# Hyena mixer of a two-layer hybrid block on Trainium2: its first loads moved ahead of attention's, its GpSimd operations moved to VectorE

## The chip, the cores and the metric

The kernel runs on one core of one Trainium2 chip. The metric is the device time of one execution in microseconds (us). The engines are named PE (TensorE), DVE (VectorE), ACT (ScalarE), POOL (GpSimd) and SP (SyncE, which here issues the loads and stores).

## The reference, cut to what matters

Two layers, 1024 latent tokens and 256 context tokens of width 1024, all in float32. In each layer an input projection feeds four mixers side by side: gated DeltaNet (gdn), Hyena, HGRN2 (hgrn) and differential attention. Their outputs are joined, projected, and an MLP follows. In the last layer the context tokens give no output, so its Hyena has the latent part alone. The part that is changed:

```python
def long_conv_bidir(u, h_fwd, h_bwd, skip):
    n, ch = h_fwd.shape
    kern = jnp.concatenate([h_fwd, jnp.zeros((1, ch), jnp.float32), jnp.flip(h_bwd[1:], axis=0)], axis=0)
    kf = jnp.fft.rfft(kern, n=2 * n, axis=0)
    uf = jnp.fft.rfft(u.astype(jnp.float32), n=2 * n, axis=1)
    y = jnp.fft.irfft(uf * kf, n=2 * n, axis=1)[:, :n]
    return (y + u.astype(jnp.float32) * skip.astype(jnp.float32)).astype(u.dtype)

def hyena_mixer(p_lat, p_ctx, conv_w, filt_params, decay, skip, want_ctx):
    def run(t):
        v, x1, x2 = _split(conv_centred(t, conv_w), [W_GROUP] * 3)
        h = hyena_filters(t.shape[1], *filt_params, decay)
        z = x1 * long_conv_bidir(v, h[:, 0, 0], h[:, 1, 0], skip[0])
        return x2 * long_conv_bidir(z, h[:, 0, 1], h[:, 1, 1], skip[1])
    return run(p_lat), (run(p_ctx) if want_ctx else None)
```

## The kernel before, in words

**Stages of a layer.** `run` builds a layer from generators. Each yields a number after every piece of work, its rough cost, and `mix(lead, fill, ratio)` draws as much of `fill` as `ratio` times what `lead` has yielded. The stages: norm and input projection; gdn with the projection as filler; hgrn as lead with `rest()` as filler; attention as lead with what is left of `rest()`; then the tail (output projection and MLP). The instructions are issued in the order in which the generators write them, with a scheduler of the framework that keeps each engine's queue in a fixed order; each engine works through its own queue in order, and so does SP with its DMAs. An instruction that waits holds up all behind it on its engine.

**The filler.** `rest()` is the end of the projection, then attention's first loads (`next(at[0])`), then the first two loads of `mods` (`next(m2)`), then `weave(hyena, m2)`: Hyena, and between its pieces the blocks 16 to 47 of the adaLN parameters. In layer 0 the first blocks of the next layer's parameters and its Hyena filters follow.

**Attention's loads.** `attn` takes a head in four pairs of `q<-dq` and `k<-dk` loads of 64 partitions x 1280 (L1159), eight in all; the next head's are issued at the start of the present one. Its scores are `psc` at L1199.

**mods.** Each block of 128 columns loads a weight tile `modw` (L342, 512 KB, two buffers) and multiplies it with the conditioning vectors: eight matmuls `pmod` (L364), then transposes `pmodT` (L350).

**hgrn.** Its tiles load `k<-khf`, `k<-khb`, `q<-hq`, `it<-i`, `lf` (L1035 to L1043). Its products are `psc` at L1090 and L1096, `po`, `pkv`, `pexp`, and `pfin` at its end.

**Hyena.** `hyena(l)` does a circular convolution by a DFT whose tokens are split into R phases: part "c" (256 context tokens, R = 2, layer 0 alone), then part "l" (1024 latent tokens, R = 4). For a part it loads the bases `bf` and `bi` (L1313; 2 MB each for "l"), the input `u<-yv` (L1457), for each of the two orders a gate `xg` (L1460), and for each block of 128 frequencies the filter's spectrum `ks` (L1476). Both parts use the same buffers. The work for one block of "l": transposes `put` (L1470, once an order), `pF` (L1319, the forward products), a butterfly over phases to `X` (L1497 to L1504), the complex product with `ks` (L1506 to L1511), a second butterfly (L1517 to L1527), `py` (L1534, the way back) and the updates of `u` (L1538 to L1542). There are eight such blocks in the kernel, and two of "c". `V` is DVE and `G` is POOL:

```python
V.tensor_mul(t1, X[:, :, 0], ks[:, :, 0])
G.tensor_mul(t2, X[:, :, 1], ks[:, :, 1])
V.tensor_mul(Y[:, :, 1], X[:, :, 0], ks[:, :, 1])
V.tensor_mul(X[:, :, 0], X[:, :, 1], ks[:, :, 0])
V.tensor_sub(Y[:, :, 0], t1, t2)
V.tensor_add(Y[:, :, 1], Y[:, :, 1], X[:, :, 0])
```

## Time and profile before

| what | value |
|---|---|
| three runs | 4753.67, 4756.74, 4767.21 us; median 4756.74 |
| span of the profiled execution | 4754.4 us |
| that execution's own time | not listed apart from the span; the span lies 2.3 us under the median |
| PE busy | 4150.7 us, 87% |
| DVE busy | 2304.5 us, 48% |
| ACT busy | 1622.4 us, 34% |
| POOL busy | 1079.8 us, 23% |
| HBM read, written | 343.83 MB, 109.48 MB |

The span is one execution of the whole program. The busy times are sums over it, so they say nothing of one stage. In time order: layer 0 has its hgrn up to about 1130 us, its attention from there to about 1640 and its tail to about 2640; layer 1 has hgrn up to about 3620, attention to about 3920, then the tail.

### The profile page before, as it was taken

The page shows a single profiled execution, that of the slowest core. Times are in us where ns is not written, and L with a number is a line of the kernel's source. Part 1 is how long each engine was busy: PE and PEld are TensorE (multiplying, and loading weights), DVE is VectorE, ACT ScalarE, POOL GpSimd, SP SyncE. Part 2 cuts the span into 40 slices and gives each one's busy share as a digit, 9 for nine tenths or more (in the row PEclk, how much of TensorE's full clock was granted, in tenths as well). Part 3 has the DMA queues.
Part 4 walks back from the last instruction along what each step waited for, and adds up shares of the span by engine and source line. Part 5 has one row for each costly group of instructions (what it writes and reads, how often), then busy time and mean ns, then how long its engine had stood idle before and what let it go on. Part 6 is the DMA issues. An engine that isn't in the chain of part 4 may idle for free. (4 is left out here: it accounts for less than half of the span.)

```text
span 4754.4 us, 81740 instructions
## 1 busy us (share of the span) xinstructions
PE 4150.7 (87%) x33446; PEld 3297.6 (69%) x33446; DVE 2304.5 (48%) x4533; ACT 1622.4 (34%) x3165; POOL 1079.8 (23%) x1101
## 2 busy tenths in 40 slices
PE   5977999856578899999999998899847779999999
PEld 2866877644455678888888676677635566788887
DVE  6566556646687333222222567456647873322222
ACT  3454414423335332222122455514413463321222
POOL 1121120000211423333333121111001104433333
PEclk7998999877788899999999999899967889999999
DMA  5236633324224411111111325634342234211112
GB/s 193 91 87 174 187 104 115 97 96 139 87 83 157 149 56 49 40 41 36 41 40 48 103 84 152 193 106 123 98 141 71 86 115 129 66 50 49 48 49 87
DMA packets 381499, 458.65 MB, mean 96 GB/s; under 512 B 137251, under 2 KB 244387, under 8 KB 379076
## 3 DMA queue, kind: packets, MB, share of 16 engines
q1 hardware_dynamic: 379300, 448.43, 30.2%
q0 software_dynamic: 1824, 4.98, 0.4%
q8 instruction: 264, 4.33, 0.4%
q14 instruction: 111, 0.91, 0.1%
HBM read 343.83 MB, written 109.48 MB: 95 GB/s over the span
## 5 line engine op out<-in xcount | busy, mean ns | idle before, releaser
L256 POOL TENSOR_TENSOR wlo<-wraw,whi 128x512 fp32r<-128x512 f32 x360 | 476.7, 1329 | 804.9 <-ACT whi L255 793.0
L255 ACT CAST whi<-wraw 128x512 fp32r<-128x512 f32 (+1 forms) x480 | 296.9, 620 | 955.1 <-PE pt L261 806.8
L1600 DVE SCALAR_TENSOR_TENSOR tx<-pt,mod,tx 128x512 f32<-128x512 f32 (+1 forms) x360 | 250.9, 697 | 710.0 <-PE pt L262 708.5
L262 PE MATMUL pt<-hh,wlo 128*128 128x512 f32 (+1 forms) x1280 | 472.6, 369 | 4.8 <-POOL wlo L256 4.8
L262 PE MATMUL pt<-fh,wlo 128*128 128x512 f32 (+1 forms) x1280 | 473.9, 370 | 0.0
L261 PE MATMUL pt<-fl,whi 128*128 128x512 f32 (+1 forms) x1280 | 472.8, 369 | 0.0
L260 PE MATMUL pt<-fh,whi 128*128 128x512 f32 (+1 forms) x1280 | 472.7, 369 | 0.0
L260 PE MATMUL pt<-hh,whi 128*128 128x512 f32 (+1 forms) x1280 | 472.1, 369 | 0.0
L261 PE MATMUL pt<-hl,whi 128*128 128x512 f32 (+1 forms) x1280 | 472.0, 369 | 0.0
L1636 DVE TENSOR_TENSOR f<-f 128x512 f32<-128x512 f32 (+1 forms) x160 | 151.9, 951 | 623.3 <-ACT f L1635 619.6
L260 PE MATMUL pproj<-hh,whi 128*128 128x512 f32 (+1 forms) x960 | 371.6, 387 | 8.3 <-ACT u L489 6.4
L261 PE MATMUL pproj<-hl,whi 128*128 128x512 f32 (+1 forms) x960 | 362.6, 378 | 0.0
L262 PE MATMUL pproj<-hh,wlo 128*128 128x512 f32 (+1 forms) x960 | 360.7, 376 | 0.0
L261 PEld LDWEIGHTS pt<-fl,whi 128*128 128x128 f32 x1280 | 240.4, 188 | 56.3 <-issue 13.0
L256 POOL TENSOR_TENSOR fl<-f,fh 128x512 fp32r<-128x512 f32 (+1 forms) x160 | 190.6, 1192 | 390.5 <-ACT fh L255 390.5
L262 PEld LDWEIGHTS pt<-hh,wlo 128*128 128x128 f32 x1280 | 241.6, 189 | 46.6 <-POOL wlo L256 5.6
L260 PEld LDWEIGHTS pt<-fh,whi 128*128 128x128 f32 x1280 | 240.5, 188 | 43.4 <-issue 2.3
L262 PEld LDWEIGHTS pt<-fh,wlo 128*128 128x128 f32 x1280 | 240.5, 188 | 43.1 <-issue 1.5
L261 PEld LDWEIGHTS pt<-hl,whi 128*128 128x128 f32 x1280 | 241.8, 189 | 41.0 <-issue 0.8
L260 PEld LDWEIGHTS pt<-hh,whi 128*128 128x128 f32 x1280 | 241.7, 189 | 40.8 <-ACT whi L255 0.3
L260 PEld LDWEIGHTS pproj<-hh,whi 128*128 128x128 f32 x960 | 186.5, 194 | 48.4 <-issue 8.7
L1201 ACT ACTIVATE p<-psc,mx 128x1280 f32<-128x1280 f32 (+1 forms) x144 | 178.0, 1238 | 120.7 <-DVE mx L1200 71.0
(377 smaller groups left out, 8357.1 us busy)
## 6 DMA issues: line engine op xcount, KB each, us to landing
wraw<-mlp_w SPq DMA_DIRECT2D x296, 256.0 KB
modw<-mod_w SPq DMA_DIRECT2D x80, 512.0 KB
wraw<-w_cm SPq DMA_DIRECT2D x88, 256.0 KB
wraw<-w_out SPq DMA_DIRECT2D x64, 256.0 KB
kv<-kvd SPq DMA_DIRECT2D x40, 256.0 KB
k<-dk SPq DMA_DIRECT2D x32, 320.0 KB
bfl<-c_hyfl SPq DMA_DIRECT2D x4, 2048.0 KB
modw<-mod_w SPq DMA_DIRECT2D x4, 2048.0 KB
```

Of the source, the lines that this page charges most:

```text
L255: (hi_eng or nc.scalar.copy)(hi, src)
L256: (lo_eng or nc.gpsimd).tensor_tensor(lo, src, hi.bitcast(F32), ALU.subtract)
L260: nc.tensor.matmul(ps, wh, xh, start=start, stop=False)
L261: nc.tensor.matmul(ps, wh, xl, start=False, stop=False)
L262: nc.tensor.matmul(ps, wl, xh, start=False, stop=stop)
L1201: nc.scalar.activation(p[j], A, AF.Exp, bias=mx[:, j:j + 1], accum_out=sm[:, j:j + 1])
L1600: nc.vector.scalar_tensor_tensor(xm, p, G[:, m, v:v + 1], xm, ALU.mult, ALU.add)
L1636: nc.vector.tensor_mul(f, f, f)
```

## The change

`hyena` gets a first part, up to a new `yield 0`, that issues the first loads of both parts at once: `sk`, and for each part `bf`, `u`, the first `ks`, `bi` and the first `xg`, each into a buffer of its own (`uc`/`ul`, `xgc`/`xgl`, `ksc`/`ksl`). The buffers `t1` and `t2` go. `rest()` takes that first part ahead of attention's loads and of `mods`, then yields 3.0, so that hgrn runs three units ahead before Hyena's work begins. All operations on POOL in `hyena` go to DVE. The complex product writes into `Y` and `X` in place. Four butterflies of 512 become two of 1024, and for "l" the result is in `Y`. Comments are gone, so line numbers shift (`put` is L1487 after, `u` L1466, `xg` L1454, `ks` L1459, `py` L1548, the stores `o<-u` L1558).

```diff
@@ -1446,19 +1446,36 @@
         gp = es.enter_context(tc.tile_pool(name=f"hy{l}", bufs=1, side="right", reuse_waits="tile"))
         sk = gp.tile([128, 4], F32, tag="sk", name="sk")
         nc.sync.dma_start(sk, self.i["hysk"][l])
-        V, G = nc.vector, nc.gpsimd
-        for nm, tok0, n, a, R in (("c", SEQ, CTX, 1, 2), ("l", 0, SEQ, 2, 4)):
-            if (l, nm) not in self.KS:
-                continue
+        V = nc.vector
+        parts = [p for p in (("c", SEQ, CTX, 1, 2), ("l", 0, SEQ, 2, 4)) if (l, p[0]) in self.KS]
+        def gate(nm, od, tok0, n):
+            xg = gp.tile([128, 2, n], F32, tag="xg" + nm, name="xg")
+            nc.sync.dma_start(xg, S["y1" if od == 0 else "y2"][:, :, tok0:tok0 + n])
+            return xg
+        def spectrum(nm, od, k, R):
+            ks = gp.tile([128, R, 2, 256], F32, tag="ks" + nm, name="ks")
+            nc.sync.dma_start(ks, self.KS[l, nm][:, od, k])
+            return ks
+        got = {}
+        for nm, tok0, n, a, R in parts:
+            bf = self.basis(gp, "f", nm)
+            u = gp.tile([128, 2, n], F32, tag="u" + nm, name="u")
+            nc.sync.dma_start(u, S["yv"][:, :, tok0:tok0 + n])
+            ks = spectrum(nm, 0, 0, R)
+            bi = self.basis(gp, "i", nm)
+            got[nm] = bf, bi, u, gate(nm, 0, tok0, n), ks
+        yield 0
+        for nm, tok0, n, a, R in parts:
             tk = slice(tok0, tok0 + n)
             pn = n // R
-            bf, bi = self.basis(gp, "f", nm), self.basis(gp, "i", nm)
-            u = gp.tile([128, 2, SEQ], F32, tag="u", name="u")[:, :, :n]
-            nc.sync.dma_start(u, S["yv"][:, :, tk])
+            bf, bi, u, xg, ks = got[nm]
             for od in range(2):
-                xg = gp.tile([128, 2, SEQ], F32, tag="xg", name="xg")[:, :, :n]
-                nc.sync.dma_start(xg, S["y1" if od == 0 else "y2"][:, :, tk])
+                if od:
+                    xg = gate(nm, od, tok0, n)
                 ut = gp.tile([128, 2, 4, 256], F32, tag="ut", name="ut")
                 for ai in range(a):
                     for b0 in range(0, R, 2):
@@ -1472,19 +1489,16 @@
                         nc.scalar.copy(ut[:, ai, b0:b0 + 2], pv)
                         yield 0.2
                 for k in range(a):
-                    ks = gp.tile([128, 4, 2, 256], F32, tag="ks", name="ks")[:, :R]
-                    nc.sync.dma_start(ks, self.KS[l, nm][:, od, k])
+                    if od or k:
+                        ks = spectrum(nm, od, k, R)
                     X = gp.tile([128, 4, 2, 256], F32, tag="X", name="X")[:, :R]
                     Y = gp.tile([128, 4, 2, 256], F32, tag="Y", name="Y")[:, :R]
-                    t1 = gp.tile([128, 4, 256], F32, tag="t1", name="t1")[:, :R]
-                    t2 = gp.tile([128, 4, 256], F32, tag="t2", name="t2")[:, :R]
                     def F(b):
                         p = self.big("pF").rearrange("p (r c) -> p r c", r=2)
                         for ri in range(2):
                             self.fourier(bf, ut, a, ri, k, b, p[:, ri])
                         return p
-                    Z = X
                     if R == 2:
                         nc.scalar.copy(Y[:, 0], F(0))
                         p = F(1)
@@ -1496,31 +1510,31 @@
                             p = F(b + 2)
                             V.tensor_add(Y[:, 2 * b], X[:, b], p)
                             V.tensor_sub(Y[:, 2 * b + 1], X[:, b], p)
-                        G.tensor_add(X[:, 0], Y[:, 0], Y[:, 2])
+                        V.tensor_add(X[:, 0], Y[:, 0], Y[:, 2])
                         V.tensor_sub(X[:, 2], Y[:, 0], Y[:, 2])
                         V.tensor_add(X[:, 1, 0], Y[:, 1, 0], Y[:, 3, 1])
                         V.tensor_sub(X[:, 1, 1], Y[:, 1, 1], Y[:, 3, 0])
-                        G.tensor_sub(X[:, 3, 0], Y[:, 1, 0], Y[:, 3, 1])
-                        G.tensor_add(X[:, 3, 1], Y[:, 1, 1], Y[:, 3, 0])
+                        V.tensor_sub(X[:, 3, 0], Y[:, 1, 0], Y[:, 3, 1])
+                        V.tensor_add(X[:, 3, 1], Y[:, 1, 1], Y[:, 3, 0])
                     yield 1
-                    V.tensor_mul(t1, X[:, :, 0], ks[:, :, 0])
-                    G.tensor_mul(t2, X[:, :, 1], ks[:, :, 1])
+                    V.tensor_mul(Y[:, :, 0], X[:, :, 0], ks[:, :, 0])
                     V.tensor_mul(Y[:, :, 1], X[:, :, 0], ks[:, :, 1])
-                    V.tensor_mul(X[:, :, 0], X[:, :, 1], ks[:, :, 0])
-                    V.tensor_sub(Y[:, :, 0], t1, t2)
-                    V.tensor_add(Y[:, :, 1], Y[:, :, 1], X[:, :, 0])
+                    V.tensor_mul(X[:, :, 0], X[:, :, 1], ks[:, :, 1])
+                    V.tensor_mul(X[:, :, 1], X[:, :, 1], ks[:, :, 0])
+                    V.tensor_sub(Y[:, :, 0], Y[:, :, 0], X[:, :, 0])
+                    V.tensor_add(Y[:, :, 1], Y[:, :, 1], X[:, :, 1])
                     if R == 2:
+                        Z = X
                         V.tensor_add(Z[:, 0], Y[:, 0], Y[:, 1])
                         V.tensor_sub(Z[:, 1], Y[:, 0], Y[:, 1])
                     else:
-                        c = [t.rearrange("p a c -> p (a c)").rearrange("p (s r c) -> p s r c", s=2, r=2) for t in (t1, t2)]
-                        V.tensor_add(c[0][:, 0], Y[:, 0], Y[:, 2])
-                        G.tensor_add(c[1][:, 0], Y[:, 1], Y[:, 3])
-                        V.tensor_sub(c[0][:, 1], Y[:, 0], Y[:, 2])
-                        V.tensor_sub(c[1][:, 1], Y[:, 1], Y[:, 3])
-                        c1, d1 = c[0][:, 1], c[1][:, 1]
-                        G.tensor_add(Z[:, 0], c[0][:, 0], c[1][:, 0])
-                        V.tensor_sub(Z[:, 2], c[0][:, 0], c[1][:, 0])
+                        Z = Y
+                        V.tensor_add(X[:, 0:2], Y[:, 0:2], Y[:, 2:4])
+                        V.tensor_sub(X[:, 2:4], Y[:, 0:2], Y[:, 2:4])
+                        V.tensor_add(Z[:, 0], X[:, 0], X[:, 1])
+                        V.tensor_sub(Z[:, 2], X[:, 0], X[:, 1])
+                        c1, d1 = X[:, 2], X[:, 3]
                         V.tensor_sub(Z[:, 1, 0], c1[:, 0], d1[:, 1])
                         V.tensor_add(Z[:, 1, 1], c1[:, 1], d1[:, 0])
                         V.tensor_add(Z[:, 3, 0], c1[:, 0], d1[:, 1])
@@ -1545,9 +1559,9 @@
                         yield 1
         es.close()
     def tail(self, l, xp):
-        """leaves the residual stream in the tiles of xp"""
         nc, tc, S = self.nc, self.tc, self.S
         full = l < DEPTH - 1
         toks = T if full else SEQ
@@ -1790,11 +1804,13 @@
                         yield from project
                         rs.close()
                         at.append(self.attn(l, qs.enter_context(pool("daf", side="right"))))
-                        next(at[0])
                         with pool("mods", side="right") as mp:
-                            m2 = self.mods(l, range(16, 48), mp)
-                            next(m2)
-                            yield from weave(self.hyena(l), m2, RM[l])
+                            hy, m2 = self.hyena(l), self.mods(l, range(16, 48), mp)
+                            for g in (hy, at[0], m2):
+                                next(g)
+                            yield 3.0
+                            yield from weave(hy, m2, RM[l])
                             if full:
                                 yield from self.mods(l + 1, range(16), mp)
                         if full:
```

**SP's queue, layer 0, where attention's first loads are issued.** Before (`sk` to `xg` are Hyena's part "c", `o_0` and what follows is hgrn's):

```order
L1159 DMA k_11271<-dk_109 64x1x1280 x2
L342 DMA modw<-mod_w 128x1024 x2
L1448 DMA sk<-hysk 128x4
L1313 DMA bfc<-c_hyfc 128x512
L1313 DMA bic<-c_hyic 128x512
L1457 DMA u<-yv_100 128x2x256
L1460 DMA xg<-y_0_101 128x2x256
L1672 DMA o_0_119<-fg 128x256
L1672 DMA o_0_120<-fg 128x256
L1476 DMA ks<-ksc_130 128x1024
L342 DMA modw<-mod_w 128x1024
L1038 DMA k<-khf_104 128x2x128
```

And with the change, where the rows `sk` to `xg` of "c" stand just ahead of these, behind the first two q loads:

```order
L1313 DMA bfl<-c_hyfl 128x4096
L1466 DMA u<-yv_100 128x2x1024
L1459 DMA ks<-ksl_129 128x2048
L1313 DMA bil<-c_hyil 128x4096
L1454 DMA xg<-y_0_101 128x2x1024
L1159 DMA k_11293<-dk_109 64x1x1280 x2
L1159 DMA q_11296<-dq_108 64x1x1280 x2
L1159 DMA k_11299<-dk_109 64x1x1280 x2
L342 DMA modw<-mod_w 128x1024 x2
L1686 DMA o_0_119<-fg 128x256
L1686 DMA o_0_120<-fg 128x256
L1038 DMA k<-khf_104 128x2x128
```

Attention's `k` and `q`, `modw` and hgrn's `k<-khf` now stand behind all first loads of both parts, where Hyena's "c" loads alone stood behind attention's.

**PE's queue at those places, layer 0 and layer 1.** Layer 0, before, at the first transposes of part "c":

```order
L1115 MATMUL po<-S_7394,X 64x128 x2
L1117 MATMUL po<-it,A_7390 64x64 x4
L1470 MATMUL put<-c_ident,u 128x128 x4
L364 MATMUL pmod<-modw,cst 32x128 x8
L1319 MATMUL pF<-ut,bfc 128x256 x4
L364 MATMUL pmod<-modw,cst 32x128 x8
L1090 MATMUL psc<-X 32x32 x8
```

Layer 0 with the change:

```order
L1123 MATMUL pkv<-it,kd 64x64 x8
L1487 MATMUL put<-c_ident,u 128x128 x2
L1117 MATMUL po<-it,A_7390 64x64 x4
L1115 MATMUL po<-S_7394,X 64x128 x2
L1117 MATMUL po<-it,A_7390 64x64 x4
L364 MATMUL pmod<-modw,cst 32x128 x8
L1319 MATMUL pF<-ut,bfc 128x256 x4
L1090 MATMUL psc<-X 32x32 x4
```

Two `put` already stand further ahead, two here; `pmod` is behind them and ahead of hgrn's next `psc`. Layer 1, before:

```order
L1055 MATMUL pexp<-lmat,lfT 128x512 x4
L1470 MATMUL put<-c_ident,u 128x128 x4
L364 MATMUL pmod<-modw,cst 32x128 x8
L1470 MATMUL put<-c_ident,u 128x128 x12
L1076 MATMUL pkd<-c_ident,X 128x128
L1319 MATMUL pF<-ut,bfl 128x256 x16
L1076 MATMUL pkd<-c_ident,X 128x128
L1090 MATMUL psc<-X 32x32 x8
```

Layer 1 with the change:

```order
L1117 MATMUL po<-it,A_29841 64x64 x4
L1487 MATMUL put<-c_ident,u 128x128
L1055 MATMUL pexp<-lmat,lfT 128x512 x2
L1487 MATMUL put<-c_ident,u 128x128 x3
L1055 MATMUL pexp<-lmat,lfT 128x512 x2
L364 MATMUL pmod<-modw,cst 32x128 x8
L1487 MATMUL put<-c_ident,u 128x128 x6
L1076 MATMUL pkd<-c_ident,X 128x128 x2
L1090 MATMUL psc<-X 32x32 x8
```

The first `put` has moved ahead of `pexp`, `pmod` stands behind four of them, and the `pF` that stood ahead of hgrn's `psc` have moved behind it. From here to attention's first scores there were 32 `pF`, 16 `py` and 40 `pmod` matmuls, and now there are 16, 8 and 24; the rest stands within attention.

**SP's queue in layer 0's attention, at the loads of the second head.** Before:

```order
L1159 DMA q_12562<-dq_108 64x1x1280 x2
L1159 DMA k_12565<-dk_109 64x1x1280 x2
L1159 DMA q_12568<-dq_108 64x1x1280 x2
L1159 DMA k_12571<-dk_109 64x1x1280 x2
L1544 DMA o_0_117<-u 128x256
L342 DMA modw<-mod_w 128x1024
L1544 DMA o_0_118<-u 128x256
L1460 DMA xg<-y_0_101 128x2x1024
L342 DMA modw<-mod_w 128x1024
L1457 DMA u<-yv_100 128x2x1024
```

With the change:

```order
L1159 DMA q_12503<-dq_108 64x1x1280 x2
L1159 DMA k_12506<-dk_109 64x1x1280 x2
L1159 DMA q_12509<-dq_108 64x1x1280 x2
L1159 DMA k_12512<-dk_109 64x1x1280 x2
L342 DMA modw<-mod_w 128x1024 x3
L1558 DMA o_0_117<-u 128x256
L342 DMA modw<-mod_w 128x1024
L1558 DMA o_0_118<-u 128x256
```

`u<-yv` and `xg` are gone from here, and three `modw` stand directly behind the head's eight loads. On PE the second `pmod` after the first scores, which reads the first of these, stands behind 11 groups of scores; before, the first `put` of part "l" stood behind 15.

## Rows read from the trace of the kernel before

**Rows 1.** The page's head and its busy times.

```profile
span 4754.4 us, 81740 instructions
...
PE 4150.7 (87%) x33446; PEld 3297.6 (69%) x33446; DVE 2304.5 (48%) x4533; ACT 1622.4 (34%) x3165; POOL 1079.8 (23%) x1101
```

**Rows 2.** Windows: from:to, length; busy us of PE, PEld, DVE, ACT, POOL; PEclk; DMA.

```profile
1020.00:1030.00 10.00, 3.20 (x20) 2.56 (x20) 3.89 (x13) 0.51 (x2) 0.00 (x0) 0.58 0.13 53
...
3490.00:3500.00 10.00, 0.00 (x0) 0.00 (x0) 0.00 (x0) 0.00 (x0) 0.00 (x0) 0.50 1.00 242
...
3700.00:3800.00 100.00, 74.40 (x567) 58.08 (x565) 86.47 (x102) 49.25 (x90) 20.81 (x23) 0.90 0.22 75
...
1180.00:1200.00 20.00, 0.00 (x0) 0.00 (x0) 0.00 (x0) 0.00 (x0) 0.00 (x0) 0.50 0.53 141
```

**Rows 3.** Timeline of PE, layer 0: start, length, operation [idle before, releaser].

```profile
1058.98 1.13 PE L1470 MATMUL put<-c_ident,u 128*128 128x128 f32 x4 [32.19 <-DMA u<-yv]
...
1068.38 0.33 PE L1090 MATMUL psc<-X 64*32 64x32 f32 x16 [4.08 <-DVE X L1071]
...
1133.51 2.50 PE L1199 MATMUL psc<-k,q 128*128 128x512 f32 x6 [0.68 <-ACT fg L1670]
...
1205.68 2.90 PE L1470 MATMUL put<-c_ident,u 128*128 128x128 f32 x12 [33.26 <-DMA u<-yv]
```

**Rows 4.** Timeline of PE, layer 1, hgrn.

```profile
3521.98 1.13 PE L1470 MATMUL put<-c_ident,u 128*128 128x128 f32 x4 [49.40 <-DMA u<-yv]
3523.03 1.08 PE L364 MATMUL pmod<-modw,cst 128*32 128x128 f32 x16
...
3623.01 2.50 PE L1199 MATMUL psc<-k,q 128*128 128x512 f32 x6 [0.67 <-ACT fg L1670]
```

**Rows 5.** Timeline of SP's queue, layer 0, and attention's first load of layer 1.

```profile
995.81 0.57 SPq L1159 DMA_DIRECT2D q<-dq  x1
...
1043.40 1.65 SPq L1457 DMA_DIRECT2D u<-yv  x1
...
1061.61 0.52 SPq L1038 DMA_DIRECT2D k<-khf  x1
...
1139.75 1.11 SPq L1159 DMA_DIRECT2D q<-dq  x2
...
1178.22 1.46 SPq L342 DMA_DIRECT2D modw<-mod_w  x1
...
1199.29 0.58 SPq L1457 DMA_DIRECT2D u<-yv  x1
...
3446.20 0.55 SPq L1159 DMA_DIRECT2D q<-dq  x1
```

**Rows 6.** Groups of PE by line, 1068 to 1134 us: busy, mean ns | idle before.

```profile
L364 PE MATMUL pmod<-modw,cst 128*32 128x128 f32 x64 | 3.5, 350 | 3.3 <-DVE mod L351 3.3
```

**Rows 7.** Groups of PE by line, 3521 to 3623 us.

```profile
L1319 PE MATMUL pF<-ut,bfl 128*128 128x256 f32 x64 | 16.2, 413 | 0.0
L1534 PE MATMUL py<-bil,X 128*128 128x256 f32 x32 | 10.3, 462 | 0.0
```

**Rows 8.** Groups of POOL by line and shape, whole span.

```profile
L1507 POOL TENSOR_TENSOR t<-X,ks 128x1024 f32<-128x1024 f32 x8 | 22.8, 2856 | 4.1 <-DVE X L1502 2.6 <-DVE oT L1242 1.0 <-ACT wT L1223 0.5
...
L1499 POOL TENSOR_TENSOR X<-Y 128x512 f32<-128x512 f32 x8 | 10.5, 1309 | 135.1 <-DVE Y L1497 135.1
```

**Rows 9.** Groups of DVE by line and shape, whole span.

```profile
L1508 DVE TENSOR_TENSOR Y<-X,ks 128x1024 f32<-128x1024 f32 x8 | 17.8, 2219 | 0.0
...
L1500 DVE TENSOR_TENSOR X<-Y 128x512 f32<-128x512 f32 x8 | 10.8, 1356 | 0.0
L1510 DVE TENSOR_TENSOR Y<-t,t 128x1024 f32<-128x1024 f32 x8 | 9.7, 1212 | 0.0
...
L1523 DVE TENSOR_TENSOR X<-t,t 128x512 f32<-128x512 f32 x8 | 5.4, 678 | 1.2 <-POOL t L1518 1.2
...
L1526 DVE TENSOR_TENSOR X<-t,t 128x256 f32<-128x256 f32 x8 | 3.3, 411 | 0.0
```

## The prediction, made before the changed kernel ran

> **What bounds the kernel now.** I read the page first: TensorE (PE) is busy for 87% of a 4754.4 us span [rows 1]. That is a mean over stages. The windows come next, because the change lives where PE is *not* full: in the recurrence (hgrn) and attention of each layer, where Hyena is woven in as filler. In attention VectorE (DVE) is the busiest engine, 86.47 of 100 us against PE's 74.40 [rows 2], and there are stretches in which nothing runs at all: the 20 us from 1180 and the 10 us from 3490 show 0.00 on every compute engine [rows 2]. PE's timeline says what ended them. In layer 0 PE stood 32.19 us and then 33.26 us for Hyena's u, each time at `put` [rows 3]; in layer 1 once, 49.40 us [rows 4]. Together 114.8 us, 2.4% of the span: the prize, if loads alone were late.
>
> SP's timeline says why they were late. Attention's eight q and k loads are issued from 995.81, and u only at 1043.40 [rows 5]. While they run, the DMA engines are busy for a share of 0.13 and move 53 GB/s [rows 2]: two engines' worth of sixteen. Each load is 64 x 1280 floats, 0.33 MB, so eight of them need 2.6 MB / 53 GB/s = 49 us. Whatever all sixteen engines carry, and stands behind them, has pieces on those two. Hyena's loads do use all: share 1.00 at 242 GB/s [rows 2].
>
> **Part 1: the loads go ahead of attention's.** In layer 0, u of the context part now has only two q loads (12 us) and its basis in front of it, so it lands near 1012 and the 32.19 us at `put` go. What is late next? The order shows `pmod` right behind `put` in PE's queue, and its weights, with hgrn's k<-khf, on SP behind *all* of Hyena's loads and the remaining attention loads. Before, SP issued k<-khf at 1061.61 [rows 5], and PE's next scores began at 1068.38, 4.08 us after they had to wait for DVE [rows 3]. Now 8.9 MB (1.6 MB of the context part, 7.3 MB of the latent) instead of the 0.8 MB that stood ahead of u lie in front of them. The 8.1 MB more cost 33 us at 242 GB/s; at the rate of one of the two slow engines (53/2 = 26 GB/s each, so 424 GB/s for sixteen) 19 us. I take 27, between them, as the bases ran at the first rate and the rest has no row of its own. PE restarts at 1058.98 + 27 = 1086 instead of 1058.98, its scores near 1090 instead of 1068.38: **+22 us**. From there to attention's first scores at 1133.51 [rows 3] were 65 us; the order leaves less filler in that stretch: `put`, a `pF` pair, the transposes and two of four `pmod`, an estimated 5 us (the four `pmod` take 3.5), and the 3.3 us that a `pmod` stood there [rows 6], so **-8 us**. Bounds: +8 and +25 for the two together.
>
> The second wait of layer 0. Before, PE reached `put` at 1172.4 and stood until u, issued at 1199.29, had landed at 1205.68 [rows 3, 5]. Now u of the latent part has long landed and `put` comes early, but a `pmod` stands at about the 11th group of scores, and the modw that it reads is issued behind the next head's eight loads, where before o<-u stood (SP came to modw at 1178.22) [rows 5]. Those loads start 6 us after attention does (1139.75 against 1133.51) and take 49 us; with 4 to 7 us for modw itself it lands some 62 us after attention's start, while PE gets there after some 29. It stands for 33 us again, with four groups of scores fewer done than before but ten us sooner: **0**, between -33 (modw in time) and +5.
>
> Layer 1. Attention's loads start at 3446.20 [rows 5], Hyena's are the latent part's alone. u lands near 3475 and the 49.40 us at `put` go. But `pmod` stands four `put` later in PE's queue, and its modw lands behind 49 us of attention loads and 7.3 MB of Hyena's, near 3527; before, `pmod` started at 3523.03 [rows 4]. hgrn's k<-khb is behind it too, so PE cannot go on elsewhere: **+5 us**. After that the order leaves 16 of 32 `pF`, 8 of 16 `py` and two `pmod` fewer ahead of attention's first scores (3623.01 before [rows 4]): half of 16.2 us and half of 10.3 us [rows 7], with the `pmod` and their transposes some **-17 us**. That work comes back inside attention. For PE there is room (74.40 of 100 us); its DVE part, some 10 us, meets an engine at 86.47 [rows 2]: **+8 us** of it shows, between 0 and 10.
>
> **Part 2: GpSimd's operations on VectorE.** Seven GpSimd groups, from L1507 down, leave, for instance eight adds of 128x512 at 1309 ns and eight products of 128x1024 at 2856 [rows 8]. The same shapes on DVE take 678 and 1210 to 1212 ns when they run alone (L1523, L1510) [rows 9]. But DVE operations that run *beside* GpSimd take about twice as long: L1500, 128x512, 1356; L1508, 128x1024, 2219 [rows 9]. So DVE gives back what it takes on. Before, a latent block's 16 rows (L1500 to L1527) sum to 16.2 us. After, by shape: four 512-wide at 0.68 (L1523), eight 256-wide at 0.41 (L1526), six products and sums and two wide butterflies of 1024 at 1.21 (L1510) [rows 9]: 2.7 + 3.3 + 9.7 = 15.7 us. Eight blocks: **-4 us**, all on DVE. Other DVE operations that happen to run beside those GpSimd ones gain too, 1 us a block by the same doubling: **-8 us**, between 0 and -12, as some of it lies where DVE waits anyway. The in-place product needs no work more; its chain is longer by no instruction.
>
> The Trainium skill's "GPSIMD Engine Reference", section 4.1, says that two-input elementwise work belongs on VectorE, GpSimd being about twice as slow: the pair 1309 and 678 ns agrees. Its section 1 says that the two share SBUF interfaces, with contention when VectorE has two SBUF inputs: L1500 and L1523 agree, and the price in the sum is that of these rows. By the first rule without the second, VectorE would simply gain half of the moved time, which is rival C.
>
> **Part 3: order at the ends.** The filler that hgrn gave up reaches further: layer 0's last filter transforms stand wholly behind the last attention product, and layer 1 ends with three `pmod` there instead of one: **+3** and **+2 us**, between 0 and +8, as PE's next work (the tail's weights) waits behind them.
>
> **Sum.** +22 - 8 + 0 + 5 - 17 + 8 - 4 - 8 + 5 = +3 us, against 4754.4: 4757. The runs' median, 4756.74, is 2.3 above that span, within their spread. Since the bound of the second wait reaches much further down (-33) than up (+5), I take 4 us off: **4755 us**. Of the 114.8 us of waits, then, nearly all come back under another name: `pmod` for modw in place of `put` for u.
>
> **Rivals.**
> *A, the second wait does go.* modw for the `pmod` at the 11th scores is in time, because SP's queue is shorter (o<-u and xg no longer hold it up) or PE gets there later. For it: before, SP took from 1178.22 to 1199.29 over modw, o<-u and xg until it came to u [rows 5]. Against: u issued at 1199.29 needed only 6 us, so it was the place in the queue, and modw's is behind eight loads. Price: -33 on the sum, 4722 us; if the DVE work that comes back in layer 1 hides as well, 4714.
> *B, slower: hgrn's loads pay and nothing is given back.* The mechanism is SP's queue in layer 0: k<-khf behind 8.9 MB. If hgrn's tiles, not the filler, set the 65 us to attention, the -8 fails, and in layer 1 the -17 likewise; then +22 + 5 + 0 + 5 - 12 (DVE) + 8 = +28: 4782 us. It decides when less than a third of the removed filler time shows as time. For it: PE waits there for DVE X and others, not only for itself (4.08 us) [rows 3]. Against: DVE loses filler as well.
> *C, slower: VectorE becomes the bound.* If the stretching at L1500 and L1508 is not GpSimd's doing, DVE gains a 512, two 256, a 1024 and a 512-wide operation per block: 0.68 + 0.82 + 1.21 + 0.68 = 3.4 us, and loses nothing. About six of the eight blocks lie in attention: +20, and the -12 fall away: 4787 us. Against it: the same shape has both durations in one function [rows 9].
> That the change does not do what it says can't be had here: the order shows the loads ahead.
>
> **How the numbers follow.** Forecast 0.46 (its own range 4737 to 4773), A 0.28, B 0.18, C 0.08. A difference below 0.3%, 14 us, can't be told from none: 4742 to 4771. The forecast gives 0.08 faster, 0.35 same, 0.03 slower; A 0.28 faster; B 0.02 same and 0.16 slower; C 0.08 slower. Sum: **faster 0.36, same 0.37, slower 0.27**. The range 4710 to 4785 takes in A, the forecast and B, and leaves out C and the ends of A and B.
>
> **What would show it.** Right: no wait at `put`; a wait of 50 us or more at a `pmod` for modw near 1030 to 1086, another of some 30 in attention of layer 0, one of about 50 near 3475 to 3527; attention's first scores near 1147 and 3611; DVE's 128x512 and 128x1024 rows of hyena at 0.68 and 1.21 us throughout. A is right if no `pmod` wait over 10 us stands in layer 0's attention. B is right if attention starts after 1153 in layer 0 and not before 3620 in layer 1. C is right if DVE's total rises above 2304.5 us [rows 1]. The forecast is wrong altogether if PE runs on between 1030 and 1080, which would mean that SP's order does not set the landing.

## The result, and the profile after

The changed kernel takes 4798.3 us in the median of four runs (4796.9 to 4800.8); the kernel before took 4756.2 us in the runs beside it. The ratio is 1.0090, with a 95% interval of 1.0076 to 1.0105: 42 us slower. The forecast was 4755 us, with 4710 to 4785 as its range, so the time lies outside it. The profiled execution has a span of 4799.0 us, 44.6 more than that of before [rows 1].

The page of the profile after, its busy times and the chain that ended last:

```profile
span 4799.0 us, 81680 instructions
...
PE 4155.5 (87%) x33446; PEld 3304.2 (69%) x33446; DVE 2291.7 (48%) x4567; ACT 1621.5 (34%) x3165; POOL 999.9 (21%) x1051
...
PE 27%; DVE 4%; DMA 3%; ACT 2%; SPq 1%; issue 1%; POOL 0%; ACTq 0%; DVEq 0%; POOLq 0%
PE pt L262 5%; PE pt L261 5%; PE pt L260 5%; DMA modw<-mod_w 2%; PE pproj L260 1%; PE pproj L261 1%; PE pproj L262 1%; DVE mx L1200 1%; DMA k<-dk 1%; ACT p L1201 1%; SPq L1159 1%; PE pvn L936 1%; PE pvn L939 0%; PE pav L1233 0%; PE psc L1199 0%
```

VectorE's total *fell* by 12.8 us, from 2304.5 [rows 1], although GpSimd gave up 80 us of work (1079.8 to 999.9). The chain that ended last now names two loads, modw and k<-dk.

The timeline of PE after, layer 0 from hgrn to the tail (start, length, operation, idle before and its releaser), answers to [rows 3]:

```profile
1015.98 0.70 PE L1487 MATMUL put<-c_ident,u 128*128 128x128 f32 x2 [15.85 <-DMA u<-yv]
...
1077.04 1.08 PE L364 MATMUL pmod<-modw,cst 128*32 128x128 f32 x16 [39.17 <-DMA modw<-mod_w]
...
1081.77 0.27 PE L1090 MATMUL psc<-X 64*32 64x32 f32 x8
...
1147.61 2.48 PE L1199 MATMUL psc<-k,q 128*128 128x512 f32 x6
...
1211.17 1.08 PE L364 MATMUL pmod<-modw,cst 128*32 128x128 f32 x16 [30.79 <-DMA modw<-mod_w]
...
1557.27 1.70 PE L1233 MATMUL pav<-wT,vt 128*64 128x128 f32 x8
...
1644.04 0.47 PE L260 MATMUL pt<-oh,whi 128*128 128x512 f32 x1 [1.05 <-ACT oh L255]
```

And layer 1, which answers to [rows 4]:

```profile
3515.36 0.49 PE L1487 MATMUL put<-c_ident,u 128*128 128x128 f32 x1 [9.72 <-DMA u<-yv]
...
3557.45 1.08 PE L364 MATMUL pmod<-modw,cst 128*32 128x128 f32 x16 [39.24 <-DMA modw<-mod_w]
...
3640.28 1.53 PE L1199 MATMUL psc<-k,q 128*128 128x512 f32 x6
...
3698.45 6.05 PE L1548 MATMUL py<-bil,Y 128*128 128x256 f32 x16 [11.02 <-DVE Y L1536]
...
3949.02 2.40 PE L1233 MATMUL pav<-wT,vt 128*64 128x128 f32 x40
...
3966.01 1.08 PE L364 MATMUL pmod<-modw,cst 128*32 128x128 f32 x16 [3.33 <-DMA modw<-mod_w]
...
3968.75 1.20 PE L260 MATMUL pt<-oh,whi 128*128 128x512 f32 x2
```

The forecast had no wait for u left in hgrn and one of 50 us at `pmod` in each layer; the waits for u have shrunk to 15.85 and 9.72 us, and PE stops soon after them at `pmod`, 39.17 us in hgrn of layer 0, 30.79 in its attention and 39.24 in hgrn of layer 1. SP's queue shows where modw and hgrn's loads came to stand, 57 and 68 us behind attention's first load (before, k<-khf was 65.8 us behind it [rows 5], but what was queued ahead of it was 8.1 MB less):

```profile
994.55 0.58 SPq L1159 DMA_DIRECT2D q<-dq  x1
...
998.05 0.57 SPq L1466 DMA_DIRECT2D u<-yv  x1
...
1052.04 7.40 SPq L342 DMA_DIRECT2D modw<-mod_w  x2
...
1062.52 3.95 SPq L1038 DMA_DIRECT2D k<-khf  x1
...
3478.03 0.55 SPq L1159 DMA_DIRECT2D q<-dq  x1
```

To split the difference, four more rows of the kernel before, the last product of attention and the first of the tail in each layer:

```profile
1543.92 1.12 PE L1233 MATMUL pav<-wT,vt 128*64 128x128 f32 x8
...
1616.42 0.50 PE L260 MATMUL pt<-oh,whi 128*128 128x512 f32 x1 [1.02 <-ACT oh L255]
...
3913.72 2.40 PE L1233 MATMUL pav<-wT,vt 128*64 128x128 f32 x40
...
3924.04 0.77 PE L260 MATMUL pt<-oh,whi 128*128 128x512 f32 x1 [0.35 <-ACT oh L255]
```

From these marks come six stages: hgrn (from attention's first q load to attention's first scores), attention (to the end of its last product), and what stands behind attention (to the tail's first product). In us, each from one profiled execution; the last three rows are experiments told below. The 3.0 is the number in the line `yield 3.0`, the three units of cost by which Hyena's work is put off; filler is what is woven between the pieces of a stage. The profiled execution of the run without the 3.0 lies 12 us under that run's median and that of the run with it alone 5 under, so sums of such rows are good to some 10 us.

| kernel | hgrn 0 | attention 0 | behind 0 | hgrn 1 | attention 1 | behind 1 |
|---|---|---|---|---|---|---|
| before | 137.7 | 411.5 | 71.4 | 176.8 | 293.1 | 7.9 |
| changed | 153.1 | 411.4 | 85.1 | 162.2 | 311.1 | 17.3 |
| difference | +15.4 | -0.1 | +13.7 | -14.6 | +18.0 | +9.4 |
| changed, without the 3.0 | 149.2 | 403.2 | 68.8 | 172.4 | 290.3 | 8.2 |
| before, with the 3.0 | 128.3 | 423.2 | 85.5 | 144.4 | 304.6 | 17.6 |
| changed, more filler in attention | 153.2 | 447.7 | 44.1 | 161.4 | 292.6 | 7.3 |

The differences sum to 41.8 of the 44.6 us; the rest lies between the layers (+4.2 in layer 0's tail and layer 1's projections, a stretch that differs by as much between kernels whose code there is the same) and in an earlier start. So what hgrn lost in layer 0 it won in layer 1, and the loss is in attention of layer 1 and *behind* attention in both layers. The equal length of layer 0's attention hides two changes that cancel, as the row without the 3.0 shows: 8.3 us shorter with the loads in front and the work on VectorE, 8.2 longer with the work put off.

### The profile page after: what moved, and what is told of

Read it like the earlier page. It is cut to its first block, busy times and chain, and to the rows that moved or that the text cites. A ratio compares the mean times of both kernels' runs of the same rounds, so it can differ in the third digit from the quotient of the medians.

```text
span 4799.0 us, 81680 instructions
## 1 busy us (share of the span) xinstructions
PE 4155.5 (87%) x33446; PEld 3304.2 (69%) x33446; DVE 2291.7 (48%) x4567; ACT 1621.5 (34%) x3165; POOL 999.9 (21%) x1051
## 5 line engine op out<-in xcount | busy, mean ns | idle before, releaser
L261 PEld LDWEIGHTS pt<-hl,whi 128*128 128x128 f32 x1280 | 241.8, 189 | 41.1 <-issue 0.8
```

The costliest lines, as they stand in the source:

```text
L261: nc.tensor.matmul(ps, wh, xl, start=False, stop=False)
```

## The experiments

All were timed beside the kernel before, in 4 to 10 executions each; its median in those runs was 4758 to 4763 us, so ratios are compared, and medians are given beside them.

**GpSimd back.** The changed kernel with the seven groups of operations on GpSimd again:

```diff
-V.tensor_add(X[:, 0], Y[:, 0], Y[:, 2])
+G.tensor_add(X[:, 0], Y[:, 0], Y[:, 2])
...
-V.tensor_add(X[:, 0:2], Y[:, 0:2], Y[:, 2:4])
-V.tensor_sub(X[:, 2:4], Y[:, 0:2], Y[:, 2:4])
+V.tensor_add(X[:, 0], Y[:, 0], Y[:, 2])
+G.tensor_add(X[:, 1], Y[:, 1], Y[:, 3])
...
```

> The changed kernel, with the seven groups of Hyena's elementwise operations back on GpSimd (the loads, the buffers, the order and the in-place product stay). Theory Q (the queues: 42 us come from the order, the three units and the loads in front, nothing from the engines): the stretched VectorE rows come back, so 4798 plus 5 to 12, about 4805 us. Rival E (the engines: PE waits longer at py since VectorE alone now does the whole chain; those waits grew by 15 us in layer 0 and 24 us in layer 1): the waits at py fall back to 15 us in all and the time to about 4765 us.

Measured: 4798.8 us, ratio 1.0084 (1.0061 to 1.0107). The same as the changed kernel. PE's waits at `py` fell from 53 to 26 us over both layers, and the time did not follow: they are taken by other waits when they go. Rival E falls; theory Q's 5 to 12 us more did not show, but the interval is too wide to rule them out. VectorE's total was 2283.5 us here, 8.2 less than in the changed kernel: of its rows, a butterfly of 128x512 is stretched again (1330 ns), the products of 128x1024 are not (1207 to 1225 ns).

**VectorE alone.** The kernel before with the changed arithmetic of `hyena`, and nothing else of the change:

```diff
-G.tensor_mul(t2, X[:, :, 1], ks[:, :, 1])
+V.tensor_mul(X[:, :, 0], X[:, :, 1], ks[:, :, 1])
...
```

> The kernel before, with the changed arithmetic alone (all of Hyena's elementwise operations on VectorE, in place, wide butterflies); loads, buffers and order as before. Theory Q: 5 to 12 us less than before, about 4748 us, waits at put unchanged (32, 33 and 49 us). Rival E: 20 to 40 us more than before, 4780 to 4795 us, with PE's waits at py near 50 us in all.

Measured: 4745.0 us, ratio 0.9972 (0.9958 to 0.9987), so 13 us faster than before. Of the three parts, the loads in front, the units and VectorE, this is the one that pays by itself. VectorE's operations run at their lone durations (128x1024 in 1212 to 1216 ns), in the changed kernel too (groups of VectorE by line and shape, busy and mean ns):

```profile
L1521 DVE TENSOR_TENSOR Y<-X,ks 128x1024 f32<-128x1024 f32 x8 | 9.7, 1217 | 0.0
...
L1514 DVE TENSOR_TENSOR X<-Y 128x512 f32<-128x512 f32 x8 | 5.5, 683 | 0.0
```

They answer to L1508 with 2219 and L1500 with 1356 ns [rows 9].

**Without the three units.** The changed kernel, one line less:

```diff
-                            yield 3.0
```

> The changed kernel without the yield of 3.0 in front of Hyena. Theory Q, first form (the three units push the filler back: behind attention the filters of layer 0 stand 14 us longer, the last blocks of mods in layer 1 9 us longer, and Hyena's work in layer 1 moves into attention, 18 us): 4798 - 35 to 40, about 4760 us; PE stops at put or pmod for loads as long as in the changed kernel or longer. Second form (the loads in front of attention's cost it): the time stays within 10 us of 4798. Rival E: within 10 us of 4798, waits at py near 50 us.

Measured: 4761.6 us, ratio 0.9996 (0.9981 to 1.0011), no different from before. So with the line `yield 3.0` the ratio is 1.0090, without it 0.9996: the loss against the kernel before goes with that line. Its row in the table shows where: behind layer 0's attention 16.3 us less, attention of layer 1 20.8 less, behind it 9.1 less, attention of layer 0 8.2 less, hgrn of layer 0 3.9 less; against that hgrn of layer 1 takes 10.2 more. The stops at `pmod` are about as long as in the changed kernel, so they are not the loss. PE's timeline of this run, the stop in each layer's hgrn:

```profile
1076.88 1.08 PE L364 MATMUL pmod<-modw,cst 128*32 128x128 f32 x16 [42.33 <-DMA modw<-mod_w]
...
3526.59 1.08 PE L364 MATMUL pmod<-modw,cst 128*32 128x128 f32 x16 [37.96 <-DMA modw<-mod_w]
```

Counted from the issue of attention's first load, they end 83.1 and 78.9 us later; in the changed kernel 82.5 and 79.4.

**mods' loads first.** The changed kernel:

```diff
-for g in (hy, at[0], m2):
+for g in (m2, hy, at[0]):
```

> The changed kernel with the first two loads of mods issued ahead of Hyena's and attention's; all else as changed. If the stop at pmod itself costs (39.2 us in each layer's hgrn): both go and the time falls by 40 to 70 us, to about 4740 us. If hgrn's own loads (k<-khf, k<-khb), which still stand behind everything, are as late (my reading of the order): the stop moves on to hgrn's psc and the time falls by less than 15 us, to about 4790 us.

Measured: 4783.5 us, ratio 1.0049 (1.0028 to 1.0070), 15 us less than the changed kernel by the medians, 20 by the ratios. The stop moved on, as the second reading had it. PE's timeline of this run, layer 0, hgrn:

```profile
1082.43 0.43 PE L1090 MATMUL psc<-X 64*32 64x32 f32 x14 [42.88 <-DVE X L1071]
```

42.88 us at hgrn's own scores instead of 39.17 at `pmod`, ending at 1082.43 instead of 1077.04. In layer 1 the stop is 32.4 us, at hgrn's `pkd`, where the changed kernel stood 9.72 and 39.24 us; hgrn takes 149.4 us there instead of 162.2, the largest part of the gain; of the other stages, attention took 9.2 us more in layer 0 and 5.2 less in layer 1.

**The three units alone.** The kernel before, one line more:

```diff
                             next(m2)
+                            yield 3.0
                             yield from weave(self.hyena(l), m2, RM[l])
```

> The kernel before with the yield of 3.0 in front of Hyena alone (loads, buffers and engines as before). If the three units by themselves are the loss (work postponed to the end of each layer's attention): 35 to 40 us above before, with the stretch behind the last attention product 14 us longer in layer 0 and 9 us longer in layer 1. If they cost only because the early loads leave nothing to do in the time won: within 12 us of before.

Measured: 4767.5 us, ratio 1.0025 (1.0011 to 1.0038): slower than before by 12 us by the ratios, 9 by the medians, at the limit of the second expectation. Behind the attentions it costs what the first expected (+14.1 and +9.7 us), and 23 us more within them; but hgrn gets 41.8 us shorter. PE's timeline of this run, hgrn of layer 0 and 1:

```profile
1057.64 0.43 PE L1090 MATMUL psc<-X 64*32 64x32 f32 x14 [32.01 <-DVE X L1071]
...
1122.76 2.48 PE L1199 MATMUL psc<-k,q 128*128 128x512 f32 x6
...
3520.45 0.69 PE L1076 MATMUL pkd<-c_ident,X 128*128 128x128 f32 x2 [27.38 <-DVE X L1063]
```

PE no longer stands at `put` for u but at hgrn's own work. In layer 0 the stop ends as long after attention's first load as before (63.2 us), but hgrn's scores come at once, at 1057.64 and not at 1068.38 [rows 3], and attention's first scores 10.8 us before 1133.51 [rows 3]; in layer 1 the stop ends 55.4 us after that load instead of 75.8.

**The loads alone.** The changed kernel without the three units and with GpSimd back, so that the loads in front and their buffers are left, with the in-place product:

```diff
-V.tensor_add(X[:, 0], Y[:, 0], Y[:, 2])
+G.tensor_add(X[:, 0], Y[:, 0], Y[:, 2])
...
-                            yield 3.0
```

> The changed kernel without the yield of 3.0 and with the seven groups of operations back on GpSimd: what is left is the loads in front, into their own buffers, and the in-place product. If the parts add up (VectorE alone gave -13 us, this plus VectorE gave 0): about 13 us above before, 4772 us, with a stop of 38 to 42 us at pmod in each layer. Rival (the engines' part is worth nothing beside the early loads, as in the pair changed kernel and GpSimd back): the same as before within 5 us, about 4760 us.

Measured: 4763.5 us, ratio 1.0009 (0.9997 to 1.0021). As the rival had it: the loads in front neither gain nor lose anything that can be told, and of VectorE's 13 us at most a part is seen beside them (1.0009 against 0.9996 with VectorE; the intervals overlap). The stops at `pmod` are 41.7 and 37.6 us, as expected.

**No units, mods' loads first.** Both edits on the changed kernel:

```diff
-for g in (hy, at[0], m2):
+for g in (m2, hy, at[0]):
...
-                            yield 3.0
```

> The changed kernel without the yield of 3.0 and with the first two loads of mods in front of Hyena's and attention's. If the gain of that order (15 us in the changed kernel) adds: 4761 - 15, about 4746 us, hence as good as VectorE alone. If it came only with the three units: 4761 us.

Measured: 4743.8 us, ratio 0.9970 (0.9957 to 0.9983): the gain adds. It lies again in layer 1's hgrn, 152.8 us against 172.4 in the run without the units; the longest stops stay, 41.1 and 35.8 us at `pmod`.

**Attention's loads spread.** As the last, and `attn`'s loads one pair of q or k at a time between other work:

```diff
+for w in weave(hy, m2, RM[l]):
+    if n < 4 and w0 >= n:
+        next(at[0])
+        n += 1
...
-                if qi == 2 and h + 1 < len(heads):
-                    load(*heads[h + 1])
+                if h + 1 < len(heads):
+                    if qi == 1:
+                        more = load(*heads[h + 1])
+                    if 2 <= qi < 6:
+                        next(more)
```

> As the run before (no yield of 3.0, loads of mods first), and attention's loads spread: the first head's four pairs one by one between the pieces of Hyena, the later heads' between their third and sixth block of queries. If the stops come from 2.6 MB on two DMA engines in one piece in front of hgrn's and mods' loads: the stops of 30 us or more go in hgrn of both layers and in attention of layer 0, and the time falls to 4680 to 4715 us. Rival (Hyena's own 8.9 MB are what hgrn waits for, or VectorE is the next limit): 4735 us or more.

Measured: 4722.2 us, ratio 0.9928 (0.9905 to 0.9952), 0.7% faster than before, 7 us short of the expected 4680 to 4715. The long stops in hgrn are gone. PE's timeline of this run:

```profile
1011.24 1.13 PE L1490 MATMUL put<-c_ident,u 128*128 128x128 f32 x4 [8.31 <-DMA u<-yv]
...
1056.73 1.12 PE L1046 MATMUL plf<-c_ident,lf 128*128 128x128 f32 x4 [7.08 <-DMA lf<-lhb]
...
1131.68 2.50 PE L1199 MATMUL psc<-k,q 128*128 128x512 f32 x6 [0.68 <-ACT fg L1687]
...
1195.55 1.08 PE L364 MATMUL pmod<-modw,cst 128*32 128x128 f32 x16 [23.18 <-DMA modw<-mod_w]
...
3503.41 1.12 PE L1046 MATMUL plf<-c_ident,lf 128*128 128x128 f32 x4 [10.05 <-DMA lf<-lhb]
```

Three stops of 30 to 40 us have become 7, 23 and 10. In attention of layer 0 the wait for modw is still 23.18 us, so that one was shortened, not removed. The edit spreads these loads and, by that, also puts most of them behind hgrn's and `mods`' loads: which of the two pays, this run does not tell apart.

**Spread, with the three units.** The last with one line back:

```diff
+                            yield 3.0
                             w0, n = 0.0, 0
```

> The run with attention's loads spread (4722 us), with the yield of 3.0 back in front of Hyena. My theory now: three units of work put off cost 35 us behind (the stretches behind attention, and attention in layer 1) and are worth something in hgrn only as far as PE doesn't stand on loads there. Here its long stops are gone, so hgrn gets 10 to 35 us shorter over both layers: 0 to 25 us above 4722. Rival (the units cost 37 us wherever they stand): about 4759 us.

Measured: 4720.0 us, ratio 0.9906 (0.9879 to 0.9932): no different from the run without. Attention starts at 1110.25 us instead of 1131.68 in layer 0, and 20 us sooner after layer 0's end in layer 1; attention and what stands behind it are 50 us longer in both layers together. Where hgrn does not stand on loads, the time won there pays for the postponed work.

**Six units.** The changed kernel:

```diff
-                            yield 3.0
+                            yield 6.0
```

> The changed kernel with a yield of 6.0 instead of 3.0. Theory: hgrn stands on the same loads, ends no sooner in layer 0 and at most 15 us sooner in layer 1, and the work put off stands behind attention: 15 us more behind layer 0's attention, 10 to 20 more in and behind layer 1's: 4798 + 15 to 35, about 4825 us. Rival (a threshold: what 3.0 does to the order is done once): 4798 within 8 us.

Measured: 4825.2 us, ratio 1.0137 (1.0112 to 1.0162), 27 us more than the changed kernel. hgrn takes 155.7 and 162.0 us, as with 3.0 (153.1 and 162.2), and its stops end at the same place, 82.9 and 79.6 us after attention's first load; behind the attentions stand 91.8 and 31.4 us, 6.7 and 14.1 more. The threshold of the rival does not show: the second three units cost 27 us, the first three 37.

**More filler in attention.** The changed kernel with other ratios of filler to attention:

```diff
-RC, RD, RM = [1.0, 1.0], [1.1, 0.8], [0.8, 0.8]
+RC, RD, RM = [1.0, 1.0], [1.25, 0.95], [0.8, 0.8]
```

> The changed kernel with more filler to a unit of attention (1.25 and 0.95 instead of 1.1 and 0.8), so that what the three units put off is done within attention. If the loss is the overhang (14 us behind attention in layer 0, 9 us in layer 1): these two stretches are again 72 and 8 us, and the time falls by 15 to 23 us, to about 4780 us. If attention has no room for it (VectorE and the waits at py): the stretches shorten and attention grows by as much, 4798 within 8 us.

Measured: 4766.0 us, ratio 1.0006 (0.9994 to 1.0019): the loss is gone, more than expected. The two layers differ. In layer 0, 41.0 us left the stretch behind attention and 36.3 came back within it (447.7 against 411.4), 5 us gained: there the work costs nearly as much inside attention as alone behind it. In layer 1 the stretch behind fell to 7.3 us and attention itself got 18.5 us *shorter* with more filler. The windows over attention and what is behind it in layer 1 (from:to, length; busy us and counts of PE, PEld, DVE, ACT, POOL; granted clock; DMA), the changed kernel:

```profile
3640.28:3968.75 328.47, 237.68 (x1939) 184.24 (x1937) 248.66 (x337) 157.27 (x289) 19.16 (x45) 0.84 0.29 95
```

and this run:

```profile
3635.99:3935.93 299.94, 228.11 (x1939) 175.57 (x1937) 245.96 (x337) 157.72 (x289) 19.09 (x42) 0.90 0.32 101
```

The same 1939 matmul records: PE is 9.6 us less busy at the higher granted clock, and stands 19 us less. The waits for modw in that stretch, 14.9 us in the changed kernel, are gone in this run. Beside them the same stretch of the kernel before, and of the run with GpSimd back:

```profile
3623.01:3924.04 301.03, 224.83 (x1849) 172.86 (x1849) 242.18 (x315) 157.00 (x287) 44.12 (x59) 0.83 0.30 99
...
3642.30:3964.38 322.08, 236.46 (x1921) 182.41 (x1919) 244.53 (x324) 157.61 (x291) 47.98 (x64) 0.86 0.30 98
```

And PE's waits at `py` in these stretches (us in total, times, longest), of the changed kernel, the run with GpSimd back and this run:

```profile
PE py L1548 <- DVE Y L1536: 24.3, 3, 11.0
...
PE py L1550 <- DVE Y L1538: 10.3, 3, 7.7
...
PE py L1548 <- DVE Y L1536: 20.3, 3, 8.7
```

The waits at `py` do not set the length of the stretch: 10.3 us go with 322.08, 20.3 with 299.94.

**Hyena's loads where they were.** The kernel before with the changed arithmetic, mods' loads first and attention's loads spread:

```diff
-                        next(at[0])
                         with pool("mods", side="right") as mp:
                             m2 = self.mods(l, range(16, 48), mp)
                             next(m2)
-                            yield from weave(self.hyena(l), m2, RM[l])
+                            for w in weave(self.hyena(l), m2, RM[l]):
...
```

> The kernel before with the changed arithmetic on VectorE, the first loads of mods in front and attention's loads spread as in the 4722 us run; Hyena's loads stay where they were, in shared buffers, without the three units. If Hyena's 8.9 MB in front are themselves a cost to hgrn: a few us below 4722, 4705 to 4722 us. If they are worth having ahead (no stop at put for u): 4725 to 4745 us, with stops at put in the trace.

Measured: 4718.6 us, ratio 0.9911 (0.9888 to 0.9934). The same as the two spread runs within their intervals. A stop at `put` for u stays in attention of layer 0:

```profile
1190.11 2.90 PE L1473 MATMUL put<-c_ident,u 128*128 128x128 f32 x12 [32.13 <-DMA u<-yv]
```

Against the first spread run, attention starts 14.3 us sooner (1117.43 against 1131.68) and takes 14.9 us more in layer 0 (417.1 against 402.2): what the early loads of Hyena win in attention they cost ahead of it, and in the time nothing of them can be told even when attention's loads are out of the way. It is the simplest of the three fastest versions, all of which beat both kernels.

## Why the prediction was wrong

Point by point, against the terms of its sum.

**The loads in layer 0, +22 - 8.** The sum was right by luck: +14.1 us at attention's first scores (1147.61 against 1133.51), where +14 was forecast, from two misses that cancel. hgrn's scores came again at 1081.77, 13.4 us later than before and not 22; counted from attention's first load, PE's stop ended 19.3 us later (82.5 against 63.2), where the prediction took 27, between the 19 and the 33 us that it had worked out for the 8.1 MB. And the -8 did not come: from hgrn's scores to attention's were 65.8 us, before 65.1. That less filler stood in this stretch did not shorten it.

**The second wait of layer 0, 0.** The wait was right: it went from `put`, 33.26 us [rows 3], to `pmod`, 30.79 us. Rival A, by which it would go, is out. That attention took 411.4 instead of 411.5 us does not prove more, since the work put off is in it (403.2 without the three units).

**Layer 1's hgrn, +5 - 17.** Right in both parts. The stop ended 79.4 us after attention's first load instead of 75.8, and from `pmod` to attention's first scores were 82.8 us instead of 100.0.

**VectorE, -4 - 8.** The total was right, 12.8 us less busy. Its worth was right for the kernel before (VectorE alone: 13 us), but in the changed kernel it can't be made out: with GpSimd back the ratio is 1.0084 against 1.0090, in intervals that leave room for some 12 us either way. If the 12 us are there, they are already inside the stages of the table.

**The postponed work, +8 and +3 + 2.** This is the step that failed. The prediction took it that work that leaves hgrn "comes back inside attention", that PE had room there and that only the VectorE part would show. It measured +18.0 us in attention of layer 1, and +13.7 and +9.4 behind the two attentions, 41 us for a forecast of 13. That is 28 of the 42 us by which the sum of +3 fell short of the 44.6 measured; most of the rest is VectorE's -12, which nothing shows on top.

Three things were overlooked. First, the filler is a fixed amount, and attention draws it at a fixed ratio (1.1 and 0.8 to a unit); what is not drawn in hgrn is not drawn faster in attention, it is left over at the end. The order had shown it ("layer 0's last filter transforms stand wholly behind"), but its price was put at a few instructions and not at three units of work in each layer. Second, the room that PE has on average was not room for this work. In layer 1, in attention and behind it together, the stretch with 90 more matmul records (1939 against 1849) is 27.4 us longer: PE is 12.9 us more busy, and stands 14.6 us more. In layer 0, drawing more of it inside attention saved only 5 of 41 us. Third, it matters when a piece comes, not only how many there are: the run with more filler does the same 1939 records of layer 1 in 28.5 us less. Which wait it is that makes the stretch long stays open: neither `py` (10.3 us with GpSimd back, and the stretch still 322.08 us) nor modw (5.6 us in the run with the units alone, and 322.24 us) goes along with its length by itself.

That the units, beside these loads, are the cause is shown by the run without them (ratio 0.9996) and by the run with six (1.0137); the loads by themselves cost nothing that can be told (1.0009), nor does the time change when the seven groups go back to GpSimd (1.0084). Why the units cost 37 us here and 9 in the kernel before (by the medians; 45 and 12 by the ratios) is shown by the stages, within the 10 us or so to which they are good: the price in and behind attention is 47 us with the old loads and 54 with the new, about the same; what differs is the return. With the old loads hgrn gets 41.8 us shorter. With Hyena's loads in front of modw and hgrn's tiles, hgrn stands on loads until the same moment whatever filler it is spared (with no units, three and six to 83.1, 82.5 and 82.9 us after attention's first load in layer 0, and to 78.9, 79.4 and 79.6 in layer 1), and gets 6.3 us shorter (153.1 and 162.2 against 149.2 and 172.4). With attention's loads spread, the return is 42 us again against a price of 50, and the times are the same.

**Rivals.** B had the right sign, a time nearer than the forecast's (4782) and half the mechanism: hgrn pays for the loads. In layer 0 nothing was given back, as B says, but attention started at 1147.61 and not after 1153, since the loads cost less. In layer 1 it started at 3640.28, not before 3620, but only because its first load came 32 us later; counted from that load, it started 14.6 us sooner, so there B fails. What made the time was lost in and behind attention, where B had the forecast's +8 and +5. C is out: VectorE's total fell.

**The loads on two DMA engines** were read rightly, from the share of 0.13 and 53 GB/s [rows 2], and the spread run fits what it meant: ratio 0.9928 with these loads moved apart, 0.9970 with them together, 20 us. It does not prove that the two engines matter, since the spread loads also come later in the queue; the same loads on sixteen engines were not tried. The Trainium skill's page "DMA: Bandwidth & Descriptors", section "Why a DMA increments its semaphore by 16 and not by 1", says that a load is spread over as many engines, up to 16, as divide the slowest dimension of both sides, and that it has landed only when all of them have reported. The sources of these loads have 2 as their slowest dimension (two parts of q, one part of k twice) and the destinations 64, so two of sixteen, 0.125: the trace agrees, with its share of 0.13 [rows 2]. The rule was left out of the forecast, which needed only the measured share.

Open, beside the wait that makes layer 1's attention long: how much of VectorE's 13 us is left beside the early loads, which would need longer runs, and how much of layer 0's 23 us that are left at `pmod` in the spread run a load still earlier would take. That was not tried.

## What to carry to other kernels

Filler has to be counted to the end: before taking any of it out of one stage, see whether the next stage draws faster or whether it ends up alone behind the last one, and price it at its full length, also inside a next stage that looks as if it had room. A load moved ahead pays only if what the engine needs next also lands sooner; otherwise the stop just changes its name, and work spared beside it returns little (6.3 us here). When a stop is shared by several waits, look for the transfer that holds the queue (here 2.6 MB at 53 GB/s) and try it in pieces or further back. And when a sum comes out, check its terms one by one: +22 - 8 came out as 14 with both terms wrong.

## What the runs showed of the hardware

The same 1939 matmul records took 237.68 us at a mean granted clock of 0.84 and 228.11 us at 0.90, in the same stretch with other stops. Here the same work took longer at the lower clock; that more standing brings the lower clock is not shown by these means, for the kernel before has 0.83 in its stretch, where PE stands 76.2 us, and the run with more filler 0.90 where it stands 71.8.

The doubling of VectorE's durations beside GpSimd went away completely when GpSimd's operations did: 1356 to 683 ns and 2219 to 1217 ns, and VectorE's total fell by 12.8 us although it took over 80 us of GpSimd's work. The price of the same move depends on what runs beside what: against the run with GpSimd back, which differs in these operations alone and where the products of 128x1024 were not stretched, VectorE's total is 8.2 us higher (2291.7 against 2283.5) for 76.6 us taken from GpSimd (1076.5 to 999.9).
